# First and fourth weight sums of an FFN quad by accumulating transfers, in two down parts as well

## The chip, the cores and the metric

One core of a Trainium2 chip runs the whole program. The time is device microseconds of one execution. Before the change it is 1014.78 us, the median of three runs (1014.74 to 1015.67).

## The reference

One layer of an encoder on 512 tokens of width 1024, all in float32: an input projection, two token mixers (a short gated convolution and a retention in both directions), a merge, and a SwiGLU FFN. The change lies in the FFN:

```
h2 = rmsnorm(x, g_ffn)
x = x + (silu(h2 @ w_ff_gate) * (h2 @ w_ff_up)) @ w_ff_down      # D_FF = 2816
return rmsnorm(x, g_final)
```

## The kernel before, in words

**Products.** A matrix product is done as three TensorE products of a high and a low part (fp32r), since each float32 number is split into a rounded high part and the rest. Weights are split on the way: ScalarE casts the high part (line 208, tile `whi`), VectorE subtracts it from the number and leaves the low part (line 209, tile `wlo`). Most large products are moreover done in Strassen's form by Winograd: the weight is cut in four quarters b11, b12, b21, b22, and seven products take the place of eight. Four of the seven need sums of quarters, one made from the other: t1 = b11+b12, t2 = t1+b22, t4 = t2+b21, and t3 = b12+b22. The token side has such forms too (a11, a12, a22, s1 to s4).

**The FFN.** Its 2816 columns are 11 blocks of 256. Ten of them are taken as five gate-and-up quads, `("g", 0)` to `("g", 4)`, which hold two blocks of gate and two of up; the eleventh is `("f", 10)`, the lone block. The down projection runs in three parts, `("d", 0)` and `("d", 4)` after quads 2 and 4, and `("d", 8)` at the end. `plan` writes the order of all weight units by hand: quads 0 and 1, quad 2, down part 0, quads 3 and 4, down part 4, the lone block, down part 8.

**Units and look-ahead.** A form of a quad comes in two units (u = 0 and 2), each of 128x1024 numbers, and each unit feeds 12 matmuls of 128x512. A quad or a down part of four thus has 14 units. `take` hands the next unit to TensorE's code and prepares units until two are ready. `load_raws` issues the loads of raw quarters on SP four units ahead into ten buffers (`raw`); `prefetch_form` makes the sum and the split. There are five buffers each of high and low parts, so that no split is made more than some four units ahead of TensorE. The queues are in order each, but the framework may place ready work of a later line ahead of earlier lines.

**Sums.** A sum is made in place in the raw buffer. VectorE does it at line 307. For quads 1 to 4, the sums t3 and t4 are instead made by an accumulating transfer: `late` notes it, and `join_late` (line 321) lets POOL issue it one unit later; the transfer adds the quarter in DRAM to the raw buffer. It must wait until the buffer's former contents have been split. For quad 0 and the output projection (`SUMMED`) all sums are prepared in DRAM far ahead.

**Orders.** `FORMS` is the order b11, t1, t2, b21, t3, t4, b22; `DOWN_FORMS` takes b21 second. In a quad, `first_a` does b11's product, `first_b` b21's, and `rest` the others, with b21's product in its middle unless `middle=False`. After the product of t3's first unit a quad calls `behind`, which makes the token-side forms of the quad before for the down part (`forms_of`, `act_forms_of`); that function returns `others`, which makes the last four of those splits. `gated` (lines 1228 to 1233) applies silu and the product of gate and up and transposes; line 1298 and its like subtract parts. `scatter` writes a quad's results to the layout of the down part with 16 transfers on SP.

**Down parts.** `down` runs `strassen(..., early=True)`. Its results of part 0 go to DRAM (`put_first`) and are added to the residual in DRAM by POOL in `add_first`, which is written ahead of down part 4 and waits for quad 4 by way of a small POOL operation, `mark` (line 1349). Part 4's results are added in DRAM by POOL (`add_y`, line 1309).

**Lone block.** `fm_quad` does its seven products in the order a11, s1, s2, a12, s3, a22, s4 and calls `ev11` after the fourth, `ev22` after the fifth. ev11 calls `behind()()`, which makes all of quad 4's token forms.

Of the kernel before, what the change touches and what calls it, by code (L numbers as in the profile page):

```python
# [39 lines left out]
NQ = NFB // 2  # L40

FF_PARTS = ((0, 4), (4, 4), (8, 3))
# [12 lines left out]
WIDTH = {"w": 512, "x": 256, "a": 512, "o": 512, "f": 256, "g": 512, "d": 512}  # L55
FORMS = ("b11", "t1", "t2", "b21", "t3", "t4", "b22")

DOWN_FORMS = ("b11", "b21", "t1", "t2", "t3", "t4", "b22")

NEEDS = {"b11": "b11", "b21": "b21", "t1": "b12", "t2": "b22"}  # L60

def plan():

    out = []

    def a(name, col):
        out.append(("c", name, 0, 8, col, 256))

    def b(name, row, nk, col, nc):
        out.append(("c", name, row, nk, col, nc))

    def quad(c0, c1):
        for name in FORMS:  # L80
            for u in (0, 2):
                out.append(("q", ("w", c0, c1), name, u, 2))

    for h in range(EARLY):
        for r in (0, 512):
            b("w_in", r, 4, (C_Q + h * QK, C_K + h * QK), 512)
    for h in range(HEADS):
        quad(C_V + h * VD, C_G + h * VD)
        if h >= EARLY:
            a("w_in", C_Q + h * QK)  # L90
            a("w_in", C_K + h * QK)
    for c in (0, 512):
        quad(C_GA + c, C_GR + c)
    for c0, c1 in ((C_XC, C_GC), (C_XC + 256, C_GC + 256), (C_GB, C_GB + 256)):
        for name in FORMS:
            out.append(("q", ("x", c0, c1), name, 0, 4))
    for s in (2, 3):
        for c in (C_XC, C_GC, C_GB):
            a("w_in", c + s * 256)
    for h in range(HEADS):  # L100
        for c in (0, 512):
            b("w_r_out", h * VD, 4, c, 512)
    for kind, name in [("a", x) for x in FORMS[:6]] + [("o", "b11"), ("a", "b22")] + [
            ("o", x) for x in ("t1", "t2", "b21", "b22", "t3", "t4")]:
        for u in (0, 2):
            out.append(("q", (kind,), name, u, 2))
    def f(q, *names):
        for n in names:
            if q == LONE:
                out.append(("q", ("f", q), n, 0, 4))  # L110
            else:
                for u in (0, 2):
                    out.append(("q", ("g", q), n, u, 2))

    def d(q0, n):
        names = FORMS if q0 + n == NQ else DOWN_FORMS
        units = [(name, u) for name in names for u in range(0, n, 2)]
        if q0 + n == NQ:

            i = units.index(("b21", 2))  # L120
            units[i:i + 3] = units[i + 1:i + 3] + units[i:i + 1]
        for name, u in units:
            out.append(("q", ("d", q0), name, u, min(2, n - u)))

    f(0, "b11", "b21")
    f(1, "b11")
    f(0, "t2", "t1", "t3", "t4", "b22")
    f(1, "t1", "t2", "b21", "t3", "t4", "b22")
    f(2, *FORMS)
    d(*FF_PARTS[0])  # L130
    f(3, *FORMS)
    f(4, *FORMS)
    d(*FF_PARTS[1])
    f(LONE, *FORMS)
    d(*FF_PARTS[2])
    return out

# [8 lines left out]
SUMMED = (("g", 0), ("o",))  # L146


def joined(quad, name):

    return quad[0] == "g" and quad not in SUMMED and name in ("t3", "t4")


def parts(quad):
# [3 lines left out]
def loads():  # L158


    out = []
    for i, x in enumerate(PLAN):
        if x[0] == "q":
            _, quad, name, u, nk = x
            need = name if quad in SUMMED else NEEDS.get(name)
            if need:
                out.append((i, quad, need, u, nk * WIDTH[quad[0]]))
    return out + [(len(PLAN), quad, "b12", u, QH) for quad in SUMMED for u in parts(quad)]
# [7 lines left out]
def block_kernel(ctx: ExitStack, tc: tile.TileContext, xw0, xw, xT, xtok, wpack, wquad, cols, decs, rot, g_ffn, g_final, out):  # L176
# [50 lines left out]
    pos = [0]  # L227
# [32 lines left out]
    def quarter(quad, name, u):  # L260
        return wquad[next(i for i, x in enumerate(QUARTERS) if x[1:4] == (quad, name, u))]
# [34 lines left out]
    def prefetch_form(quad, f, u, nk):  # L296


        n = nk * WIDTH[quad[0]]
        if quad in SUMMED:  # L300
            here, more = f, None
        else:
            here = {"t1": "b11", "t2": "b11", "t4": "b11", "t3": "b12"}.get(f, f)
            more = {"t1": "b12", "t2": "b22", "t4": "b21", "t3": "b22"}.get(f)
        t = raws[quad, here, u][:, 0:n]
        if more and not joined(quad, f):
            nc.vector.tensor_tensor(out=t, in0=t, in1=raws[quad, more, u][:, 0:n], op=ALU.add)  # L307
        hi, lo = unit()
        split(t, hi[:, 0:n], lo[:, 0:n])
        for g, after, src, add in (("t3", "t1", "b12", "b22"), ("t4", "t2", "b11", "b21")):  # L310
            if f == after and joined(quad, g):
                late.append((pos[0] + 1, raws[quad, src, u], quarter(quad, add, u), n))
        return [(hi, lo)]

    late = []
# [771 lines left out]
    def behind(i):  # L1087
        if i == 5:
            turn(0, 0)
            return  # L1090
        turn(1, 1)
        po["a"] = [bank(), bank()]
        prod_tm(4, of(M["a11"]), po["a"], True, False, lambda tt: join(tt, 0, po["a"][tt]))
        turn(0, 1)
        form(M, "s1", m32["a22"], m32["a21"], m32["a22"], ALU.subtract)
        form(M, "s2", m32["a22"], m32["a22"], m32["a11"], ALU.subtract)
# [100 lines left out]
    def lone_gated(th, g, u):  # L1197

        s = t512()
        nc.scalar.activation(s, g, AF.Silu)  # L1200
        if not lone_x:
            lone_x.extend(t512().rearrange("p (b q e t) -> p b q e t", b=2, q=1, e=2) for _ in range(2))
        for b, o in enumerate(lone_x):
            for e in range(2):
                x, y = (t.rearrange("p (e j b r) -> p e b j r", e=2, j=2, b=4)[:, e, 2 * b:2 * b + 2] for t in (u, s))
                z = o[:, :, 0, e, 64 * th:64 * th + 64].rearrange("p b (j r) -> p b j r", j=2)
                nc.vector.tensor_tensor(out=z, in0=x, in1=y, op=ALU.mult)
# [3 lines left out]
    def lone(behind):  # L1211
        got = {}

        def ev11(t):
            got.update(g=t)
            behind()()
        forms = {"a11": XF[0, 0], "a12": XF[1, 0], "a22": XF[1, 1], **{n: XF[n] for n in ("s1", "s2", "s3", "s4")}}
        fm_quad(forms, ev11, lambda ps: lone_gated(1, ps, got["u"]),
                lambda t: got.update(u=t), lambda t: lone_gated(0, got["g"], t))
        act_forms_of(LONE, 1, *lone_x)()  # L1220

    turned = {}
# [41 lines left out]
    def first_b(i):  # L1264
        b = [bank(), bank()]
        prod_tm(4, of(XF[1, 0]), b, True, True)
        for tt, p1 in enumerate(heads_of[i][1]):
            nc.vector.tensor_tensor(out=p1, in0=b[tt], in1=p1, op=ALU.add)
# [32 lines left out]
    def quad(i, behind, after=None):  # L1301
        first_a(i)
        if after:
            after()
        rest(i, behind=behind)

    first = dram.tile([S, D], F32, name="first_part")
    def add_y(t, nb, half):
# [221 lines left out]
```

## Time and profile before

| | before |
| --- | --- |
| median of three runs | 1014.78 us (1014.74 to 1015.67) |
| the profiled execution | 1016.66 us, its span 1014.4 us |
| TensorE busy | 1002.5 us, 99% |
| VectorE busy | 894.2 us, 88% |
| ScalarE busy | 547.4 us, 54% |
| GpSimd (POOL) busy | 154.3 us, 15% |
| moved by DMA | 215.87 MB, mean 213 GB/s |
| granted TensorE clock | 0.996 |

In the profile's rows a timeline line has start, duration (both us), engine, source line, operation, out<-in tiles, shapes, the count of merged instructions and, in brackets, the idle time before it and what ended it. A line of a stretch (A:B) has the length, then the busy time and count of TensorE, its weight loads, VectorE, ScalarE and POOL, then the granted clock, the mean busy share of the 16 DMA engines and GB/s. A group of issues has the least, middle and largest duration in ns, and the first and last start.

### The profile page before, as it was taken

The page shows a single profiled execution, that of the slowest core. Times are in us where ns is not written, and L with a number is a line of the kernel's source. Part 1 is how long each engine was busy: PE and PEld are TensorE (multiplying, and loading weights), DVE is VectorE, ACT ScalarE, POOL GpSimd, SP SyncE. Part 2 cuts the span into 40 slices and gives each one's busy share as a digit, 9 for nine tenths or more (in the row PEclk, how much of TensorE's full clock was granted, in tenths as well). Part 3 has the DMA queues.
Part 4 walks back from the last instruction along what each step waited for, and adds up shares of the span by engine and source line. Part 5 has one row for each costly group of instructions (what it writes and reads, how often), then busy time and mean ns, then how long its engine had stood idle before and what let it go on. Part 6 is the DMA issues. An engine that isn't in the chain of part 4 may idle for free.

```text
span 1014.4 us, 13342 instructions
## 1 busy us (share of the span) xinstructions
PE 1002.5 (99%) x4746; PEld 838.4 (83%) x4746; DVE 894.2 (88%) x1163; ACT 547.4 (54%) x736; POOL 154.3 (15%) x246
## 2 busy tenths in 40 slices
PE   9999999999999999999999999999999999999996
PEld 7888888888888998888888888888887888888884
DVE  7878898979798888697989997999988996989897
ACT  7547655553655455343452325577665555574664
POOL 0030221222122004112221200011101000003202
PEclk9999999999999999999999999999999999999998
DMA  9525587695767658839687865467677369486953
GB/s 352 189 76 184 185 289 219 206 306 177 231 191 257 222 217 276 332 131 331 154 306 257 288 233 180 127 202 231 167 228 152 139 208 267 107 248 127 274 140 104
DMA packets 60642, 215.87 MB, mean 213 GB/s; under 512 B 8928, under 2 KB 9056, under 8 KB 55968
## 3 DMA queue, kind: packets, MB, share of 16 engines
q1 hardware_dynamic: 42592, 144.73, 41.7%
q0 software_dynamic: 17696, 70.01, 25.6%
q8 instruction: 37, 0.61, 0.3%
q10 hardware_dynamic: 288, 0.29, 0.1%
q14 instruction: 29, 0.24, 0.1%
HBM read 171.21 MB, written 57.41 MB: 225 GB/s over the span
## 4 chain that ended last, share of the span: by engine, by line
PE 87%; DVE 8%; issue 2%; SPq 2%; DMA 1%; ACT 1%; POOL 0%; POOLq 0%; DVEq 0%; ACTq 0%
PE bank L445 48%; PE bank L360 10%; PE bank L361 10%; PE bank L362 10%; PE bank L401 8%; DVE wlo L209 2%; SPq L1243 2%; DVE raw L307 1%; DMA big<-turned 1%; DVE turned L1233 1%; DVE t L1229 1%; DVE t L1182 0%; DVE big L209 0%; PE bank L501 0%; ACT whi L208 0%
## 5 line engine op out<-in xcount | busy, mean ns | idle before, releaser
L208 ACT CAST whi<-raw 128x1024 fp32r<-128x1024 f32 (+2 forms) x299 | 301.8, 1028 | 239.0 <-PE bank L445 73.5
L209 DVE TENSOR_TENSOR wlo<-raw,whi 128x1024 fp32r<-128x1024 f32 (+2 forms) x300 | 350.8, 1189 | 69.6 <-ACT whi L208 68.9
L445 PE MATMUL bank<-whi,xform 128*128 128x512 f32 x1056 | 330.5, 390 | 0.0
L445 PEld LDWEIGHTS bank<-whi,xform 128*128 128x128 f32 x1056 | 198.0, 188 | 42.2 <-DVE xform L209 1.0
L445 PE MATMUL bank<-wlo,xform 128*128 128x512 f32 x528 | 205.8, 390 | 0.5 <-DVE wlo L209 0.5
L445 PE MATMUL bank<-whi,big 128*128 128x512 f32 x596 | 187.5, 390 | 0.3 <-ACT t L452 0.3
L307 DVE TENSOR_TENSOR raw<-raw 128x1024 f32<-128x1024 f32 x112 | 132.2, 1198 | 0.8
L445 PEld LDWEIGHTS bank<-whi,big 128*128 128x128 f32 x596 | 111.7, 188 | 24.5 <-ACT t L452 1.1
L445 PEld LDWEIGHTS bank<-wlo,xform 128*128 128x128 f32 x528 | 99.1, 188 | 22.1 <-DVE wlo L209 1.7
L445 PE MATMUL bank<-wlo,big 128*128 128x512 f32 x298 | 116.1, 390 | 0.1
L452 ACT COPY t<-bank 128x512 f32<-128x512 f32 x95 | 55.5, 587 | 70.8 <-PE bank L445 55.8
L360 PE MATMUL bank<-big,whi 128*128 128x512 f32 x220 | 85.7, 390 | 0.0
L362 PE MATMUL bank<-big,wlo 128*128 128x512 f32 x220 | 85.6, 389 | 0.0
L361 PE MATMUL bank<-big,whi 128*128 128x512 f32 x220 | 85.6, 389 | 0.0
L445 PEld LDWEIGHTS bank<-wlo,big 128*128 128x128 f32 x298 | 55.9, 188 | 12.0 <-DVE wlo L209 0.6
L401 PE MATMUL bank<-xform,whi 128*128 128x256 f32 x304 | 55.3, 283 | 0.2 <-ACT t L452 0.2
L360 PE MATMUL bank<-whi,big 128*128 128x512 f32 x128 | 49.8, 389 | 0.0
L361 PE MATMUL bank<-wlo,big 128*128 128x512 f32 x128 | 49.8, 389 | 0.0
L362 PE MATMUL bank<-whi,big 128*128 128x512 f32 x128 | 49.8, 389 | 0.0
L362 PEld LDWEIGHTS bank<-big,wlo 128*128 128x128 f32 x220 | 41.3, 188 | 8.7
L361 PEld LDWEIGHTS bank<-big,whi 128*128 128x128 f32 x220 | 41.3, 188 | 8.5
L360 PEld LDWEIGHTS bank<-big,whi 128*128 128x128 f32 x220 | 41.3, 188 | 8.5
(211 smaller groups left out, 1395.1 us busy)
## 6 DMA issues: line engine op xcount, KB each, us to landing
raw<-wquad SPq DMA_DIRECT2D x140, 512.0 KB, 5.2
raw<-wpack SPq DMA_DIRECT2D x42, 512.0 KB, 5.9
raw<-wquad POOLq DMA_DIRECT2D x16, 512.0 KB, 6.4
t_g<-wquad POOLq DMA_DIRECT2D x12, 512.0 KB, 7.7
z<-t POOLq DMA_DIRECT2D x24, 256.0 KB, 5.6
t_o<-wquad POOLq DMA_DIRECT2D x12, 512.0 KB, 6.7
zform<-z POOLq DMA_DIRECT2D x6, 1024.0 KB, 7.1
big<-turned SPq DMA_DIRECT2D x80, 64.0 KB, 4.5
```

Of the source, the lines that this page charges most:

```text
L208: first = (round or nc.scalar.copy)(hi, src)
L209: low_of[0] = nc.vector.tensor_tensor(out=lo, in0=src, in1=hi.bitcast(F32), op=ALU.subtract)
L307: nc.vector.tensor_tensor(out=t, in0=t, in1=raws[quad, more, u][:, 0:n], op=ALU.add)
L360: nc.tensor.matmul(ps, lh, rh, start=first, stop=False)
L361: nc.tensor.matmul(ps, lh, rl, start=False, stop=False)
L362: nc.tensor.matmul(ps, ll, rh, start=False, stop=last)
L401: nc.tensor.matmul(o, l[:, c], r[:, k], start=start and s == 0 and k == 0 and i == 0, stop=stop and k == 3 and i == 2, skip_group_check=True)
L445: nc.tensor.matmul(pss[tt], l, r[:, c], start=start and k == 0 and i == 0, stop=stop and k == n - 1 and i == 2, skip_group_check=True)
L452: nc.scalar.copy(t, ps)
L1229: nc.vector.tensor_tensor(out=s, in0=u, in1=s, op=ALU.mult)
L1233: nc.vector.transpose(t[:, :, :, j, :].rearrange("p q i r -> p i q r"), s.rearrange("p (i q c) -> p i q c", i=4, q=4)[:, :, 2 * h:2 * h + ...
L1243: nc.sync.dma_start(o[32 * q:32 * q + 32], turned[i][q // 2][32 * b:32 * b + 32, q % 2].rearrange("c i j r -> c (i j r)"))
```

## The change

For quads 1 to 4 the transfers now make t1 (b12 added to b11 after b11's split) and t4, and VectorE makes t2 and t3. The quarter b12 is loaded only for t3. The two down parts 0 and 4 do the same; before, VectorE made all their sums. Quads 2, 3 and 4 take b21 second, so `quad` calls `first_b` right after `first_a`, and its sums with the first product follow there. In the lone block the last four token forms of quad 4 are made at `ev22`, one product later than before.

```
-DOWN_FORMS = ("b11", "b21", "t1", "t2", "t3", "t4", "b22")
+EARLY_FORMS = ("b11", "b21", "t1", "t2", "t3", "t4", "b22")
+NEEDS_JOINED = {"b11": "b11", "b21": "b21", "t2": "b22", "t3": "b12"}
...
-    f(2, *FORMS)
+    f(2, *EARLY_FORMS)
     d(*FF_PARTS[0])
-    f(3, *FORMS)
-    f(4, *FORMS)
+    f(3, *EARLY_FORMS)
+    f(4, *EARLY_FORMS)
...
-def joined(quad, name):
-    return quad[0] == "g" and quad not in SUMMED and name in ("t3", "t4")
+def joined(quad):
+    return quad not in SUMMED and (quad[0] == "g" or quad[0] == "d" and quad[1] < FF_PARTS[-1][0])
+
+def needed(quad, name):
+    return NEEDS_JOINED.get(name) if joined(quad) else name if quad in SUMMED else NEEDS.get(name)
...
-        if more and not joined(quad, f):
+        if more and not (joined(quad) and f in ("t1", "t4")):
             nc.vector.tensor_tensor(out=t, in0=t, in1=raws[quad, more, u][:, 0:n], op=ALU.add)
         hi, lo = unit()
         split(t, hi[:, 0:n], lo[:, 0:n])
-        for g, after, src, add in (("t3", "t1", "b12", "b22"), ("t4", "t2", "b11", "b21")):
-            if f == after and joined(quad, g):
-                late.append((pos[0] + 1, raws[quad, src, u], quarter(quad, add, u), n))
+        add = {"b11": "b12", "t2": "b21"}.get(f)
+        if add and joined(quad):
+            late.append((pos[0] + 1, raws[quad, "b11", u], quarter(quad, add, u), n))
...
         def ev11(t):
-            got.update(g=t)
-            behind()()
+            got.update(g=t, others=behind())
...
-                lambda t: got.update(u=t), lambda t: lone_gated(0, got["g"], t))
+                lambda t: (got.update(u=t), got["others"]()), lambda t: lone_gated(0, got["g"], t))
...
         first_a(i)
         if after:
             after()
-        rest(i, behind=behind)
+        first_b(i)
+        rest(i, middle=False, behind=behind)
```

More of the change, by code (lines that the diff above doesn't have):

```diff
@@ L115, in d @@
     def d(q0, n):
-        names = FORMS if q0 + n == NQ else DOWN_FORMS
+        names = FORMS if q0 + n == NQ else EARLY_FORMS
         units = [(name, u) for name in names for u in range(0, n, 2)]
@@ L164, in loads @@
             _, quad, name, u, nk = x
-            need = name if quad in SUMMED else NEEDS.get(name)
+            need = needed(quad, name)
             if need:
```

## The prediction

> **What bounds the kernel now.** I read the page first: the busy shares, and the chain that ended last.
>
> ```profile
> span 1014.4 us, 13342 instructions
> PE 1002.5 (99%) x4746; PEld 838.4 (83%) x4746; DVE 894.2 (88%) x1163; ACT 547.4 (54%) x736; POOL 154.3 (15%) x246
> PE 87%; DVE 8%; issue 2%; SPq 2%; DMA 1%; ACT 1%; POOL 0%; POOLq 0%; DVEq 0%; ACTq 0%
> ```
>
> TensorE is busy for all but 12 us, and most of those lie before the first product and after the last. The chain still gives VectorE 8%. Which of the two sets the pace in the FFN is not seen from busy time, because matmuls are pipelined and their ends are modelled. It is seen from the distance between the starts of neighbouring matmuls. So I went through the timeline of TensorE from 691 us (first FFN product) to the end, looking for starts that lie too far apart. Undisturbed, three 128x512 matmuls take 0.68 us, 0.227 us each (770.14 to 770.82 below), and one unit of weights (12 matmuls) takes 2.72 us. In the stretch that the change touches there are four places where the starts lie further apart:
>
> ```profile
> 767.72 0.61 PE L445 MATMUL bank<-whi,xform 128*128 128x512 f32 x2
> 768.42 0.50 PE L445 MATMUL bank<-wlo,xform 128*128 128x512 f32 x1
> 768.75 0.63 PE L445 MATMUL bank<-whi,xform 128*128 128x512 f32 x2
> ...
> 770.14 0.61 PE L445 MATMUL bank<-whi,xform 128*128 128x512 f32 x2
> 770.59 0.39 PE L445 MATMUL bank<-wlo,xform 128*128 128x512 f32 x1
> 770.82 0.61 PE L445 MATMUL bank<-whi,xform 128*128 128x512 f32 x2
> 771.89 0.50 PE L445 MATMUL bank<-wlo,xform 128*128 128x512 f32 x1 [0.46 <-DVE wlo L209]
> 772.23 0.63 PE L445 MATMUL bank<-whi,xform 128*128 128x512 f32 x2
> ...
> 824.62 0.39 PE L445 MATMUL bank<-whi,big 128*128 128x512 f32 x1
> 825.32 0.50 PE L445 MATMUL bank<-whi,big 128*128 128x512 f32 x1 [0.31 <-ACT t L452]
> 825.65 0.40 PE L445 MATMUL bank<-wlo,big 128*128 128x512 f32 x1
> ...
> 886.44 0.61 PE L445 MATMUL bank<-whi,xform 128*128 128x512 f32 x2
> 887.00 0.50 PE L445 MATMUL bank<-wlo,xform 128*128 128x512 f32 x1
> 887.34 0.64 PE L445 MATMUL bank<-whi,xform 128*128 128x512 f32 x2
> ...
> 939.76 0.83 PE L445 MATMUL bank<-whi,big 128*128 128x512 f32 x2
> 940.43 0.40 PE L445 MATMUL bank<-wlo,big 128*128 128x512 f32 x1
> ```
>
> A row of x2 takes 0.45 us from its start to the next start, a row of x1 0.227. Quad 2: 0.70 for two (+0.25), 0.33 for one (+0.10), 1.07 for two (+0.62), 0.34 for one (+0.11): 1.08 us lost. Down part 0: 0.70 and 0.33 for one each, 0.57 lost. Quad 4: 0.56 for two and 0.34 for one, 0.22 lost. Down part 4: 0.67 for two, 0.22 lost. Together 2.09 us, and that is all that the quads 1 to 4 and the two down parts can return; the rest of the FFN before the last evictions runs at 0.227 us a matmul, and the change removes no matmul.
>
> Who is late in quad 2? VectorE, and it has no gap:
>
> ```profile
> 761.21 1.18 DVE L209 TENSOR_TENSOR wlo<-raw,whi 128x1024 fp32r<-128x1024 f32 x1
> 762.31 1.21 DVE L307 TENSOR_TENSOR raw<-raw 128x1024 f32<-128x1024 f32 x1
> 763.44 1.28 DVE L1298 TENSOR_TENSOR t<-bank,t 128x512 f32<-128x512 f32 x2
> ...
> 767.18 1.18 DVE L209 TENSOR_TENSOR wlo<-raw,whi 128x1024 fp32r<-128x1024 f32 x1
> 768.29 2.35 DVE L307 TENSOR_TENSOR raw<-raw 128x1024 f32<-128x1024 f32 x2
> 770.61 2.36 DVE L209 TENSOR_TENSOR wlo<-raw,whi 128x1024 fp32r<-128x1024 f32 x2
> ```
>
> L307 is the weight sum, L209 the low part of a split. Before the low part that TensorE awaits (the first of the two at 770.61, done at 771.8) stand three sums (762.31 and two at 768.29: t1's two halves and t2's first) and the eviction of the quad before. The three sums take 3.5 us.
>
> In the down parts it is ScalarE's order. A cast that waits for a sum stands between the two copies that free the banks for the next product:
>
> ```profile
> 822.32 0.59 ACT L452 COPY t<-bank 128x512 f32<-128x512 f32 x1 [2.06 <-PE bank L445]
> 823.73 1.05 ACT L208 CAST whi<-raw 128x1024 fp32r<-128x1024 f32 x1 [0.82 <-DVE raw L307]
> 824.68 0.58 ACT L452 COPY t<-bank 128x512 f32<-128x512 f32 x1
> 939.46 0.58 ACT L452 COPY t<-bank 128x512 f32<-128x512 f32 x1
> ```
>
> **The change, part by part.**
>
> Sums in the down parts. A quad of weights has four sums of two halves each. Down parts 0 and 4 go from eight VectorE sums each to four; their t1 and t4 come by transfer. Eight sums of 1.2 us, 9.6 us of VectorE, go, and with them what the cast at 823.73 and its like in down part 4 waited for. t1's two sums are done before t2's, so t2's splits too come some 2.3 us earlier. I count the 0.57 and the 0.22 as gone.
>
> Sums in quads 1 to 4. The number stays four on VectorE, four by transfer, but t2 and t3 are now VectorE's instead of t1 and t2, and b21 goes to the place of t1. In quad 2 that takes the three sums out from before the low part at 770.61: it could be done at 771.8-3.5 = 768.3, and TensorE wants it at the third matmul of its unit, 770.7 undisturbed. 2.4 us of margin where 1.1 was missing. What comes in: the two sums of first products (`first_b`, 0.6 us each as at L1298) move up to b21's end, but those wait for that product and so stand behind this low part. Quad 4 has the same order. I count 1.08 and 0.22 as gone. The t3 sums fall later, where each unit brings VectorE one low part and one sum, 2.4 us in 2.72; that is cover with little to spare, and without it they would cost what they overrun.
>
> The transfers. There were 16; now there are 24. POOL issues them and they land:
>
> ```profile
> L321 POOL DMA_DIRECT2D raw<-wquad x16: 870/873/947, 721.1 to 892.0; - x16
> DMA to landing us min/median/max: 5.3/6.4/11.2
> ```
>
> Eight more cost POOL 7 us, in which nothing of the path stands on it. Each starts when both parts of a split are done and must land before the next cast of the same buffer. This distance shrinks from six units (16.3 us) to four (10.9 us). The tightest by the rows above is t1's second half in quad 2: the low part ends at 762.4, the landing is at 767.7 to 773.6, the cast ends by 774.6 and the low part by 775.8; TensorE reaches the unit at 767.95+3x2.72 = 776.1. Even the slowest landing seen fits, by 0.3 us; with 6.4 us there are 5 us to spare. Cost zero, and 0 to 3 us for the worst case below.
>
> A page of the Trainium skill speaks against these transfers. "SBUF — State Buffer", section "A bandwidth-pool intuition that's wrong (but worth ruling out)", says that descriptors of a GpSimd-issued DMA cannot be written while VectorE holds the shared port, and gives 620 ns alone against 3100 ns beside a VectorE copy; by that ratio the issue would take 4.4 us (estimate from the page), each landing would come 3.5 us later, and quad 2's margin would be mostly used up, a gain nearer 1 us than 2. The trace does not agree for the operations here: all 16 issues took 0.870 to 0.947 us, between 721 and 892 us, where VectorE had few gaps. The chance of late landings below takes nothing from it.
>
> Loads. The loads on SP keep their number and size; b12 moves from t1's place to t3's and the b21 load forward. By the order of uses a buffer is free at least six units (16.3 us) before it is wanted in both versions. Cost zero; the bound is a unit, 2.7 us, if a load should fall behind the 16 issues of a `scatter`.
>
> Lone block. The rest of quad 4's forms (four splits and two differences) move from after its fourth product to after its fifth. It is no less work: six operations of 0.6 us, 3.6 us of VectorE, move behind that product, against splits and sums of the last down part that can come forward.
>
> ```profile
> 969.58 0.63 PE L445 MATMUL bank<-whi,big 128*128 128x512 f32 x2
> 970.41 0.50 PE L401 MATMUL bank<-xform,whi 128*128 128x256 f32 x2 [0.21 <-ACT t L452]
> 980.00:1000.00 20.00, 20.00 (x89) 16.39 (x88) 19.27 (x32) 13.21 (x24) 3.91 (x6) 1.00 0.35 53
> ```
>
> I take zero on the path, between -0.4 (TensorE waits for a copy at 969.58, 0.83 us for two matmuls instead of 0.45, and matmuls of the last down part could fill that) and +1, of which below.
>
> Sum: -1.08 -0.57 -0.22 -0.22 = -2.1 us against the profiled execution (span 1014.4 of 1016.66 us). It is a difference of stalls, so it carries over to the median: 1014.78-2.1 = 1012.7 us. Its own range comes from the lone block's -0.4 to +1 and from a 0.22 that may stay: 1012.3 to 1013.9.
>
> **The rivals.**
>
> Given back in the down parts. If ScalarE's order keeps t4's cast between the two copies, the cast now waits for a landing instead of a sum. In down part 4 the DMA engines are full then, and the low part before the transfer is this:
>
> ```profile
> 928.00:936.00 8.00, 8.00 (x37) 6.64 (x36) 8.00 (x9) 4.11 (x4) 1.79 (x2) 1.00 1.11 213
> 931.52 1.22 DVE L209 TENSOR_TENSOR wlo<-raw,whi 128x1024 fp32r<-128x1024 f32 x1
> ```
>
> It ends at 932.7, or 930.4 without t1's sums; plus 5.3 to 11.2 us the landing is at 935.7 to 941.6, the cast ends by 942.7 at the latest and the copy by 943.2 instead of 940.0. Lost: 0 to 3.2 us, so 1012.7 to 1015.9. For it: the DMA share of 1.11. Against it: with the median landing nothing is lost.
>
> Slower, through POOL's queue. In down part 4, t1's second transfer is written in the program behind the mark and the eight additions of the first part:
>
> ```profile
> 920.11 0.22 POOL L1349 TENSOR_SCALAR mark<-t 128x1 f32<-128x1 f32 x1 [27.20 <-DVE t L1229]
> 920.39 6.81 POOL L1309 DMA_DIRECT2D ydr<-first_part  x8
> 915.30 2.31 DVE L209 TENSOR_TENSOR wlo<-raw,whi 128x1024 fp32r<-128x1024 f32 x2
> 930.24 0.62 PE L445 MATMUL bank<-whi,big 128*128 128x512 f32 x2
> ```
>
> If the queue keeps that order, the transfer starts at 927.2 instead of 916.5 (its low part is the first at 915.30), lands at 933.6 (6.4) to 938.4 (11.2), and the cast ends 1.05 later. TensorE wants that unit at 930.46, at 928.6 with the gain: 6.1 to 10.9 us lost, 4 to 9 net, 1018.8 to 1023.7 us. It decides as soon as the issue comes after about 925. Against it: the queues are not in program order throughout (at 768.29 t2's first sum runs ahead of a split of t1), and the transfer is ready 3.6 us before the mark.
>
> The lone block's forms collide. VectorE is full there (19.27 of 20 us in the stretch from 980), so 3.6 us of forms for which nothing comes forward push the splits of the last down part; I let one us of that reach TensorE: 1013.7 us.
>
> Nothing happens: other work of VectorE moves into the place of the sums and TensorE waits as before, 1014.8.
>
> **How the numbers follow.** 0.2% is 2 us, about what a measurement of this kernel can tell from no change; the forecast gain sits on that line. Forecast 0.56 (0.35 of it below 1012.75), given back 0.19 (0.04 of it over 1016.8), POOL's queue 0.11, lone block 0.09, nothing 0.05. So faster 0.36 and 0.02 for a lone block that gains, 0.38; slower 0.15; within 0.47. The range leaves out POOL's queue and the far end of the giving back above, 0.13, and 0.05 below: 1011.9 to 1016.8.
>
> **What would show it.** Right: starts of matmuls 0.227 us apart through quad 2's third and fourth unit and through t3 of both down parts; sums at L307 eight fewer (112 to 104) and accumulating transfers 24; casts of t1 and t4 that wait for nothing or for a landing well ahead of TensorE; the mark on POOL behind all of t1's transfers. Wrong: a gap of TensorE that ends on a ScalarE copy with a cast waiting for a DMA ahead of it, a transfer behind the mark, or gaps in the last down part at 984 to 990 us.

## The result, and the profile after

The change is slower: 1044.03 us, the median of five runs (1040.49 to 1046.08), against 1015.27 us before (1014.74 to 1015.91). The ratio is 1.028, 95% interval 1.026 to 1.030. The prediction was 1012.7 us. The profiled execution of the change took 1040.49 us, its span 1038.7 us, 24.3 us more than the span before; it is the shortest of the five, and where the others lost up to 5.6 us more isn't seen here. Below, lines of the changed kernel are six higher than before (those from 1228 to 1298 are five higher): the sum L307 is L313, the cast L208 is L214, the low part L209 is L215, the accumulating transfer L321 is L327, TensorE's product L445 is L451, the copy out of a bank L452 is L458.

The page of the changed kernel, the group of the sums, and the waits of TensorE (line, whom it waited for: us in all, times, longest) come first, then the transfers' issues and landings:

```profile
span 1038.7 us, 13368 instructions
PE 1005.9 (97%) x4746; PEld 841.4 (81%) x4746; DVE 886.6 (85%) x1155; ACT 546.9 (53%) x736; POOL 161.4 (16%) x254
PE 75%; DVE 9%; issue 7%; DMA 6%; POOL 2%; ACT 1%; SPq 0%; POOLq 0%; DVEq 0%; ACTq 0%
L313 DVE TENSOR_TENSOR raw<-raw 128x1024 f32<-128x1024 f32 x104 | 122.6, 1198 | 4.7 <-DMA raw<-wquad 3.9
...
PE bank L451 <- ACT t L458: 21.8, 4, 11.7
...
L327 POOL DMA_DIRECT2D raw<-wquad x24: 872/873/1011, 691.7 to 944.1; - x24
  ACT whi L214: 54.8, 15
DMA to landing us min/median/max: 5.3/6.4/15.6
```

The work did what the diff says: 104 sums, 24 transfers. But the chain that ended last is 75% TensorE instead of 87%, DMA has 6% of it instead of 1%, and TensorE waits four times, 21.8 us in all, for the copy at L458 that frees a bank. ScalarE, which makes that copy, waited 54.8 us for the transfers. Summing every distance between TensorE's starts beyond the undisturbed one gives some 7 us before and 31 us after; the 24 us between them are the whole loss of the profiled execution.

TensorE at the first and the last of the four places (an undisturbed start follows 0.227 us after the one before):

```profile
783.56 0.39 PE L451 MATMUL bank<-whi,xform 128*128 128x512 f32 x1
789.40 0.79 PE L451 MATMUL bank<-whi,xform 128*128 128x512 f32 x1 [5.45 <-ACT t L458]
...
949.32 0.39 PE L451 MATMUL bank<-whi,big 128*128 128x512 f32 x1
961.36 0.80 PE L451 MATMUL bank<-whi,big 128*128 128x512 f32 x1 [11.65 <-ACT t L458]
```

783.56 and 949.32 are the last matmuls of t2's product in quad 2 and in down part 4. ScalarE's timeline at the four places (quad 2, down part 0, quad 4, down part 4), and then in quad 3, where nothing is lost:

```profile
783.54 1.04 ACT L214 CAST whi<-raw 128x1024 fp32r<-128x1024 f32 x1 [1.21 <-DMA raw<-wquad]
784.49 1.56 ACT L214 CAST big<-big 128x1024 fp32r<-128x1024 f32 x2
787.81 1.04 ACT L214 CAST whi<-raw 128x1024 fp32r<-128x1024 f32 x1 [1.76 <-DMA raw<-wquad]
788.76 1.06 ACT L458 COPY t<-bank 128x512 f32<-128x512 f32 x2
...
827.25 1.05 ACT L214 CAST whi<-raw 128x1024 fp32r<-128x1024 f32 x1 [4.12 <-DMA raw<-wquad]
831.75 1.04 ACT L214 CAST whi<-raw 128x1024 fp32r<-128x1024 f32 x1 [3.44 <-DMA raw<-wquad]
832.70 1.07 ACT L458 COPY t<-bank 128x512 f32<-128x512 f32 x2
...
905.60 1.05 ACT L214 CAST whi<-raw 128x1024 fp32r<-128x1024 f32 x1 [2.82 <-DMA raw<-wquad]
906.56 1.05 ACT L214 CAST big<-big 128x1024 fp32r<-128x1024 f32 x1
909.23 0.62 ACT L214 CAST big<-big 128x512 fp32r<-128x512 f32 x1 [1.63 <-DMA big<-turned]
909.76 1.04 ACT L214 CAST whi<-raw 128x1024 fp32r<-128x1024 f32 x1
910.71 1.06 ACT L458 COPY t<-bank 128x512 f32<-128x512 f32 x2
...
955.96 1.04 ACT L214 CAST whi<-raw 128x1024 fp32r<-128x1024 f32 x1 [13.27 <-DMA raw<-wquad]
959.78 1.04 ACT L214 CAST whi<-raw 128x1024 fp32r<-128x1024 f32 x1 [2.77 <-DMA raw<-wquad]
960.73 1.06 ACT L458 COPY t<-bank 128x512 f32<-128x512 f32 x2
...
869.04 1.06 ACT L214 CAST whi<-raw 128x1024 fp32r<-128x1024 f32 x1 [0.15 <-PE bank L451]
870.40 0.59 ACT L458 COPY t<-bank 128x512 f32<-128x512 f32 x1 [0.30 <-PE bank L451]
```

At each of the four places the two casts `whi<-raw` are t4's two units, in quad 3 the cast is the second of them (the casts of `big` are token forms). On ScalarE they stand ahead of the two copies that empty the banks of t2's product. The copies are due when that product ends; the cast ahead of them waits for the landing, and the queue is in order. In quad 3 the cast waited for no landing and the copy came on time.

Quad 4 is a mixed case. t4's second transfer landed there at 908.90, before t2's product ended. Its cast at 909.76 waited for no landing, but stood behind the cast of a token form at 909.23, which waited for quad 3's scattered results. The slowest of those 16 transfers took 6.8 us to land, against at most 3.3 us in the kernel without t4's transfer (below). The copies stood behind both casts.

The transfer starts behind t2's split. Its low parts on VectorE (the second of three, the second of four) and the issues on POOL:

```profile
776.56 3.48 DVE L215 TENSOR_TENSOR wlo<-raw,whi 128x1024 fp32r<-128x1024 f32 x3
941.34 4.62 DVE L215 TENSOR_TENSOR wlo<-raw,whi 128x1024 fp32r<-128x1024 f32 x4
...
779.26 0.89 POOL L327 DMA_DIRECT2D raw<-wquad  x1 [0.24 <-issue]
927.33 0.87 POOL L327 DMA_DIRECT2D raw<-wquad  x1 [3.61 <-DVE wlo L215]
930.37 0.22 POOL L1355 TENSOR_SCALAR mark<-t 128x1 f32<-128x1 f32 x1 [2.17 <-DVE t L1234]
944.09 0.89 POOL L327 DMA_DIRECT2D raw<-wquad  x1 [0.17 <-issue]
```

Worked out from the timelines of VectorE, POOL, ScalarE and TensorE, for t2's and t4's second unit at each place (us):

| | low part of t2 done | t4's transfer issued | t4's cast starts | last start of t2's product | next start | lost |
| --- | --- | --- | --- | --- | --- | --- |
| quad 2 | 778.90 | 779.26 | 787.81 | 783.56 | 789.40 | 5.61 |
| down part 0 | 822.35 | 822.70 | 831.75 | 829.77 | 833.33 | 3.33 |
| quad 3 | 860.62 | 861.11 | 869.04 | 871.33 | 871.56 | 0 |
| quad 4 | 901.23 | 901.58 | 909.76 | 909.41 | 911.33 | 1.69 |
| down part 4 | 943.69 | 944.09 | 959.78 | 949.32 | 961.36 | 11.81 |

At all four places with a loss TensorE goes on 1.57 to 1.59 us after t4's cast starts: the cast and one copy. So the transfer's deadline is not the use of t4 by TensorE, four units on. It is the end of t2's product, 4.3 to 7.8 us after the issue at the four places and 10.2 us in quad 3. The landings took 8.5 us in quad 2, 8.9 in down part 0, 7.3 in quad 4, 15.6 in down part 4, and 7.1 in quad 3.

How much would have been lost without the copies behind the casts? As an estimate from the table: TensorE wants t4's second unit three units (8.2 us) after t2's product ends, which is 0.23 us after its last start. That is 792.0 in quad 2, where the cast ended at 788.9, and 957.7 in down part 4, where it ended at 960.8. So t4 itself was late for TensorE in down part 4 alone, by some 3 of the 11.8 us.

### The profile page after: what moved, and what is told of

It is laid out like the page before. It is cut to its first block, busy times and chain, and to the rows that moved or that the text cites. A ratio compares the mean times of both kernels' runs of the same rounds, so it can differ in the third digit from the quotient of the medians.

```text
span 1038.7 us, 13368 instructions
## 1 busy us (share of the span) xinstructions
PE 1005.9 (97%) x4746; PEld 841.4 (81%) x4746; DVE 886.6 (85%) x1155; ACT 546.9 (53%) x736; POOL 161.4 (16%) x254
## 4 chain that ended last, share of the span: by engine, by line
PE 75%; DVE 9%; issue 7%; DMA 6%; POOL 2%; ACT 1%; SPq 0%; POOLq 0%; DVEq 0%; ACTq 0%
PE bank L451 39%; PE bank L366 10%; PE bank L368 10%; PE bank L367 10%; PE bank L407 6%; DMA raw<-wquad 6%; DVE wlo L215 3%; DVE raw L313 1%; DVE big L215 1%; DVE t L1188 1%; POOL ydr L1315 1%; ACT whi L214 1%; POOL raw L327 1%; DVE t L1294 0%; PE bank L507 0%
## 5 line engine op out<-in xcount | busy, mean ns | idle before, releaser
L214 ACT CAST whi<-raw 128x1024 fp32r<-128x1024 f32 (+2 forms) x299 | 303.9, 1029 | 297.8 <-PE bank L451 87.6
L215 DVE TENSOR_TENSOR wlo<-raw,whi 128x1024 fp32r<-128x1024 f32 (+2 forms) x300 | 351.9, 1189 | 101.0 <-ACT whi L214 100.6
L451 PE MATMUL bank<-whi,xform 128*128 128x512 f32 x1056 | 332.8, 392 | 7.0 <-ACT t L458 7.0
L451 PEld LDWEIGHTS bank<-whi,xform 128*128 128x128 f32 x1056 | 199.3, 189 | 50.3 <-ACT t L458 7.8
L451 PE MATMUL bank<-wlo,xform 128*128 128x512 f32 x528 | 206.5, 391 | 0.0
L451 PE MATMUL bank<-whi,big 128*128 128x512 f32 x596 | 189.3, 392 | 15.1 <-ACT t L458 14.8
L451 PEld LDWEIGHTS bank<-whi,big 128*128 128x128 f32 x596 | 112.8, 189 | 40.0 <-ACT t L458 15.7
L313 DVE TENSOR_TENSOR raw<-raw 128x1024 f32<-128x1024 f32 x104 | 122.6, 1198 | 4.7 <-DMA raw<-wquad 3.9
L451 PE MATMUL bank<-wlo,big 128*128 128x512 f32 x298 | 116.9, 392 | 0.0
L451 PEld LDWEIGHTS bank<-wlo,xform 128*128 128x128 f32 x528 | 99.7, 189 | 20.6
L458 ACT COPY t<-bank 128x512 f32<-128x512 f32 x95 | 54.8, 586 | 50.7 <-PE bank L451 32.7
L451 PEld LDWEIGHTS bank<-wlo,big 128*128 128x128 f32 x298 | 56.4, 189 | 11.8 <-DVE wlo L215 0.3
L327 POOL DMA_DIRECT2D raw<-wquad x24 | 21.2, 884 | 220.9 <-DVE wlo L215 209.4
L367 PEld LDWEIGHTS bank<-big,whi 128*128 128x128 f32 x220 | 41.3, 188 | 8.6
```

What stands on the lines that cost most here:

```text
L214: first = (round or nc.scalar.copy)(hi, src)
L215: low_of[0] = nc.vector.tensor_tensor(out=lo, in0=src, in1=hi.bitcast(F32), op=ALU.subtract)
L327: nc.gpsimd.dma_start(out=t[:, 0:n], in_=src[:, 0:n], accum_op=ALU.add)
L367: nc.tensor.matmul(ps, lh, rl, start=False, stop=False)
L451: nc.tensor.matmul(pss[tt], l, r[:, c], start=start and k == 0 and i == 0, stop=stop and k == n - 1 and i == 2, skip_group_check=True)
L458: nc.scalar.copy(t, ps)
```

## Experiments

Ratios are to the kernel before on the same chip, with their 95% interval. Two theories stood against each other; the letters in the expectations name variants of them, each with what it means. One: t4's transfer is issued too late for the place of its casts on ScalarE. Two: something else of the change is at fault (the transfers as such, the order of the quads, the queue of POOL, the lone block).

**Without t4's transfer.** t1 stays with the transfers, t4 goes back to VectorE.

```
-        if more and not (joined(quad) and f in ("t1", "t4")):
+        if more and not (joined(quad) and f == "t1"):
-        add = {"b11": "b12", "t2": "b21"}.get(f)
+        add = {"b11": "b12"}.get(f)
```

> The changed kernel with t1 alone made by transfer, in quads 1 to 4 and in the two down parts; t2, t3 and t4 are VectorE's. The number of VectorE's sums is then 12 higher than in the changed kernel and 4 higher than before. Theory A: no cast waits for a transfer in front of a copy with TensorE behind it, 1013 to 1017 us (some VectorE lateness may return). Theory D (t1's transfer, with 10.9 us from split to next cast, does the harm): 1030 us or more.

1014.25 us, ratio 0.9986 (0.9977 to 0.9996), 30 us below the change and as theory A had it. Its page:

```profile
span 1011.4 us, 13343 instructions
PE 97%; DVE 1%; issue 0%; ACT 0%; POOL 0%; POOLq 0%; DVEq 0%; ACTq 0%
```

The chain is 97% TensorE where it was 87%. In the quads and the two down parts no distance of TensorE's starts is over the undisturbed one by more than 0.2 us: the four stalls of before are gone, and t1's twelve transfers cost nothing. The whole loss hangs on t4's transfer: without it there is none.

**The order of the quads, with the transfers of before.** The kernel before, its quads 2 to 4 in the new order; t3 and t4 by transfer there, no transfers in the down parts.

```
-    f(2, *FORMS)
+    f(2, *DOWN_FORMS)
...
-        rest(i, behind=behind)
+        first_b(i)
+        rest(i, middle=False, behind=behind)
```

> The kernel before, with b21 second in quads 2 to 4 and its product early, as in the change; the transfers stay those of before (t3 and t4 in the quads alone), the lone block too. Theory E: t4 has four units instead of six and loses as in the kernel with the quads alone (6.5 us in quad 2, 2.2 to 2.7 in the others): 1022 to 1030 us. If t4's distance is not at fault but t1's transfer ahead of it: 1012 to 1016 us.

1028.37 us, ratio 1.0116 (1.0101 to 1.0132). TensorE's waits:

```profile
PE bank L445 <- ACT t L452: 10.6, 2, 5.9
```

6.0 us in quad 2, 4.8 in quad 4, at the same place. So in the quads it is the order that does it, without t1's transfer and without any in the down parts: with b21 taken second, t4 follows t2 two units sooner, and a transfer of t4 behind which TensorE did not stop at six units' distance stops it at four.

**The quads alone.** `joined` holds for quads only; the down parts make all sums on VectorE.

```
-    return quad not in SUMMED and (quad[0] == "g" or quad[0] == "d" and quad[1] < FF_PARTS[-1][0])
+    return quad not in SUMMED and quad[0] == "g"
```

> The changed kernel with the two down parts' sums back on VectorE; quads 1 to 4 and the lone block as changed. Theory A: the gaps in down part 0 and 4 (3.3 and 11.8, with the slow matmuls behind the second 1.5 more) go back to the 0.6 and 0.2 of before, those in quads 2 and 4 stay: about 1040.5-3.5-13.3+0.8 = 1024.5 us, 1022 to 1029. If the down parts were all of it: 1015. If the shorter distance in the quads were all of it: 1040.

1028.53 us, ratio 1.0127 (1.0111 to 1.0143). Losses of 6.5, 2.7 and 2.2 us in quads 2, 3 and 4, none in the down parts. The loss splits into about 13 us for the quads and 15 for the down parts. There the order is that of before; what is new in them is the transfer.

**Less on the DMA engines.** The mark and the eight additions of the first part are written behind down part 4.

```
-    add_first(nc.gpsimd.tensor_scalar_add(mark, gate_of[0][:, 0:1], 0.0))
     down(4, add_y)
+    add_first(nc.gpsimd.tensor_scalar_add(mark, gate_of[0][:, 0:1], 0.0))
```

> The changed kernel with the eight additions of the first part's result written behind down part 4 instead of ahead of it. Theory A with the DMA engines' crowd as the reason for the slow landings in down part 4 (12.9 and 15.6 us from issue, against 5.3 to 9.1 elsewhere): the landings fall to about 9, the gap of 11.8 us to about 5, and 1 us of slow matmuls goes: 1033 to 1037 us, with the gaps in quads 2 and 4 and down part 0 unchanged. If the loads and the scatter on the other queue make the crowd: 1040 to 1046, the landings as before.

1038.77 us, ratio 1.0228 (1.0212 to 1.0244). The two landings of t4 in down part 4 (issues at 943.5 and 944.7):

```profile
DMA to landing us min/median/max: 8.9/9.9/10.8
```

In the change they took 12.9 and 15.6 us. The loss there falls from 11.8 to 6.6 us; the other places stay (6.1, 3.3, 1.8), and a new 1.4 us appears in the last part. A landing 4.8 us shorter gives a loss 5.2 us smaller: the landing sets it. The time lies above the 1033 to 1037 us expected, since the gap fell to 6.6 us and not to 5.

**An earlier start.** t4's buffer is that of b21, and b21 is added to it right behind b21's split, four units before t2's. It leaves out t4's true sum, so its result is not the layer's; it serves for the time alone.

```
-            here = {"t1": "b11", "t2": "b11", "t4": "b11", "t3": "b12"}.get(f, f)
+            here = {"t1": "b11", "t2": "b11", "t4": "b21" if joined(quad) else "b11", "t3": "b12"}.get(f, f)
...
-        add = {"b11": "b12", "t2": "b21"}.get(f)
+        add = {"b11": "b12", "b21": "b21"}.get(f)
...
-            late.append((pos[0] + 1, raws[quad, "b11", u], quarter(quad, add, u), n))
+            late.append((pos[0] + 1, raws[quad, f, u], quarter(quad, add, u), n))
```

> The changed kernel with t4's transfer made early: it adds b21 to the raw buffer of b21 as soon as that is split, eight units ahead of t4's cast, instead of to t2 after t2's split. So t4's weights are 2 x b21 and not t4; sums on VectorE, transfers, their sizes and the order of products stay those of the changed kernel. Theory H (the harm is only that t4's landing comes after its cast's place in ScalarE's queue): no gap, 1013 to 1017 us. Theory C (24 transfers, or t4's by whatever start, crowd the DMA engines): 1030 us or more.

1026.68 us, ratio 1.0104 (1.0090 to 1.0117): between the ranges of the two theories, so neither holds alone. 17 us are back, down part 0 and quads 3 and 4 without a loss over 0.25 us. Left are 2.9 us in quad 2, where ahead of the copies stand t3's second cast, which waits for VectorE's sum, and t4's two behind it, and 4.6 us in down part 4. POOL and ScalarE there:

```profile
922.13 0.22 POOL L1355 TENSOR_SCALAR mark<-t 128x1 f32<-128x1 f32 x1 [1.14 <-DVE t L1234]
922.41 5.95 POOL L1315 DMA_DIRECT2D ydr<-first_part  x7
931.02 0.91 POOL L327 DMA_DIRECT2D raw<-wquad  x1 [0.40 <-DVE t L471]
...
944.73 1.04 ACT L214 CAST whi<-raw 128x1024 fp32r<-128x1024 f32 x1 [6.58 <-DMA raw<-wquad]
945.68 1.06 ACT L458 COPY t<-bank 128x512 f32<-128x512 f32 x2
```

Here the second transfer stands behind the mark and the additions on POOL, starts at 931.02 and lands 13.6 us later. That is the mechanism of the prediction's rival of POOL's queue, for t4 instead of t1.

**A later use.** In quads 2 to 4 and the down parts t4 changes places with b22, form and product.

```
-EARLY_FORMS = ("b11", "b21", "t1", "t2", "t3", "t4", "b22")
+EARLY_FORMS = ("b11", "b21", "t1", "t2", "t3", "b22", "t4")
...
```

> The changed kernel with the order b11, b21, t1, t2, t3, b22, t4 in quads 2 to 4 and in down parts 0 and 4: the product of t4 comes last, so that its transfer has six units (16.3 us) after t2's split instead of four (10.9). Theory E (the loss is the short time from t2's split, itself only 1 to 5 us ahead of TensorE, to t4's cast; ScalarE's queue only decides which copy stands behind it): the gaps in quad 2, down part 0 and quad 4 go, down part 4 keeps up to 6 us of its 11.8 since its landings took 13 to 16 us: 1013 to 1022 us. Theory F (a t4 transfer does the same harm wherever its product stands, since the framework places its cast just as early): 1030 us or more.

1036.55 us, ratio 1.0199 (1.0177 to 1.0220). Its waits, and ScalarE in down part 4:

```profile
PE bank L451 <- ACT t L458: 10.9, 2, 8.8
...
953.76 1.04 ACT L214 CAST whi<-raw 128x1024 fp32r<-128x1024 f32 x1 [6.17 <-DMA raw<-wquad]
959.61 1.04 ACT L214 CAST whi<-raw 128x1024 fp32r<-128x1024 f32 x1 [4.80 <-DMA raw<-wquad]
960.57 1.07 ACT L458 COPY t<-bank 128x512 f32<-128x512 f32 x2
```

This is theory F's range; E had 1013 to 1022 us. Two units (5.4 us) more give only 7.5 us back in all. In down part 4 t4's casts now stand ahead of the copies of t3's product instead of t2's, and TensorE loses 8.9 us there: the same wait, one product on. In quads 2 to 4 it waits three times, 4.0 us in all, for a subtraction of VectorE (L1303 there): it empties the bank of t1's product, which the exchanged order wants one product sooner. So this edit moves more than t4.

**The casts off ScalarE's queue.** t4's high part is made by POOL.

```
-        split(t, hi[:, 0:n], lo[:, 0:n])
+        split(t, hi[:, 0:n], lo[:, 0:n], round=nc.gpsimd.tensor_copy if f == "t4" and joined(quad) else None)
```

> The changed kernel with the casts of t4's units (quads 1 to 4, down parts 0 and 4) on POOL instead of ScalarE; transfers and their times as in the changed kernel. Theory H: ScalarE's copies wait for no landing any more; the gaps after t2's product in quad 2, down part 0 and quad 4 go; VectorE's low part still waits for the landing, in front of evictions one product later, and in down part 4 t4 itself is up to 5 us late: 1015 to 1024 us. Theory I (t4 is late for TensorE itself, whatever queue waits): 1030 us or more.

1031.63 us, ratio 1.0147 (1.0131 to 1.0162): 12 us back, yet outside theory H's 1015 to 1024.

```profile
PE bank L451 <- ACT t L458: 5.7, 2, 3.7
PE bank L451 <- POOL whi L214: 1.2, 1, 1.2
...
907.15 0.62 ACT L214 CAST big<-big 128x512 fp32r<-128x512 f32 x1 [8.03 <-DMA big<-turned]
907.68 1.07 ACT L458 COPY t<-bank 128x512 f32<-128x512 f32 x2
```

Down part 4 falls from 11.8 us to 1.4 and 1.0 at two places, though its landings took 12.4 and 14.4 us, only 0.6 and 1.2 less than in the change. So most of the 11.8 us was the wait in ScalarE's queue. The 2.4 us left are TensorE waiting for t4 itself, first for POOL's cast and then for VectorE's low part; the estimate above had 3. But the copies in quad 4 and down part 0 now stand behind another cast that waits for a DMA, a token form that waits for the scattered results (3.8 and 2.2 us lost), and 1.9 us are lost in quad 2 and 1.8 in the last part.

**The casts held behind the copies.** t4's split may start only behind the last copy out of a bank written before it; `last_copy` is noted where the copy is made. The same line was tried in four kernels more.

```
+        if f == "t4" and quad[0] in "gd" and quad not in SUMMED and quad[1] < FF_PARTS[-1][0]:
+            with tc.issue_after(last_copy[0].ins):
+                split(t, hi[:, 0:n], lo[:, 0:n])
...
```

> The changed kernel with one order added: on ScalarE the casts of t4's units stand behind the copies that free the banks of t2's product. Theory A (the loss is ScalarE's queue: t4's casts wait for their transfers in front of those copies): the gaps of TensorE after t2's product in quad 2 (5.6 us), down part 0 (3.3), quad 4 (1.7) and down part 4 (11.8) go, except that in down part 4 the second landing (at 959.7 in the changed kernel, where t4's second unit was due at 957.5) may still cost up to 4: 1012.5 to 1018 us, at or below the kernel before. Theory B (the transfers themselves are too slow, whatever stands behind them: t4 is late for TensorE): TensorE stops at t4 instead, 1030 us or more. Theory C (the added traffic slows the loads): 1035 to 1045 us.

> The kernel with t1 alone by transfer, and t4's casts held behind the copies of t2's product. With t1 alone TensorE loses no more than 0.2 us at one place in the quads and down parts, so there is nothing left to win there: 1014.25 give or take 0.7. A look for a version under both.

> The kernel before the change, with nothing changed but that t4's casts of quads 1 to 4 and of down parts 0 and 4 are held behind the copies of t2's product. Theory G: the gaps of 0.57 and 0.22 us in the down parts, where a copy stands behind a cast that waits for a sum, go: 1014.5 to 1015 against 1015.3. If other orders change with it, within 1 us of that.

> The kernel with t1 and t3 by transfer, and t4's casts (which wait for a sum of VectorE there) held behind the copies of t2's product. Theory G: the one gap of that kernel (3.3 us in quad 2, in front of a copy with a cast of t4 ahead of it) goes, 1018.23 to about 1014.5; if the late landings of t1 in quad 2 hold VectorE back by themselves, the gap moves one product on and 1017 to 1018 stays.

> The kernel with t4's product last (six units after t2's split), and t4's casts on ScalarE held behind the last copies written before them, here those of t3's product. Theory G (both count: the landing must come before TensorE wants t4, and the cast must not stand in ScalarE's queue ahead of a copy that is due before that landing): the gaps of the kernel with t4 two units later (2.3 and 1.1 in quad 2, 1.2 in quad 3, 2.3 in quad 4, 8.9 in down part 4) shrink to what a late landing costs by itself, some 3 us in down part 4: 1015 to 1022 us against 1036.55. Theory F (a t4 transfer harms wherever its cast stands): 1030 us or more.

| | without the line | with it |
| --- | --- | --- |
| the change | 1.0280 (1.0259 to 1.0302) | 1.0286 (1.0257 to 1.0315) |
| without t4's transfer | 0.9986 (0.9977 to 0.9996) | 1.0077 (1.0063 to 1.0092) |
| before | 1 | 0.9994 (0.9985 to 1.0003) |
| t1 and t3 by transfer (below) | 1.0021 (1.0012 to 1.0030) | 1.0078 (1.0065 to 1.0091) |
| t4 two units later | 1.0199 (1.0177 to 1.0220) | 1.0241 (1.0226 to 1.0255) |

Of the five forecasts with the line only that for the kernel before came true (1015.03 us); the others measured 1043.47 us (theory A: 1012.5 to 1018), 1024.01 (1014.25), 1022.97 (1014.5, or 1017 to 1018) and 1039.38 (1015 to 1022). The test is inconclusive. The line costs 9 us in the kernel without t4's transfer, where no transfer is late, though nothing in the kernel before: the held-back casts pile up, and later copies and products wait for them. The waits of the kernel without t4's transfer but with the line, where L451 has become L456 and L1297 copies the banks of t3's product:

```profile
PE bank L456 <- ACT whi L214: 5.2, 3, 2.0
PE bank L456 <- ACT t L1297: 2.9, 3, 1.0
```

In the change with the line, t4's transfers of down part 4 were issued at 947.39 and 949.20 and landed at 961.88 and 964.18; the casts now stood ahead of the copies of t3's product, and TensorE lost 11.5 us there, one product on. So the line can't tell how much of the loss is the late landing and how much the place of the casts.

**Another pair by transfer.** t1 and t3: a transfer adds b12 to b11 for t1; b12 is also loaded, at t1's place, and another transfer adds b22 to it for t3. t2 and t4 are VectorE's.

```
...
-        add = {"b11": "b12", "t2": "b21"}.get(f)
+        to, add = {"b11": ("b11", "b12"), "t1": ("b12", "b22")}.get(f, (None, None))
```

> The changed kernel with t1 and t3 by transfer (t3: b22 added to b12 as soon as that is loaded, which waits for no split) and t2 and t4 on VectorE, in quads 1 to 4 and both down parts: as many sums on VectorE and as many transfers as in the changed kernel. Theory E: no transfer hangs on t2's split, so no gap: 1011.5 to 1014.5 us, at or a little under t1 alone (1014.25), which has 12 sums more on VectorE. Theory C (24 transfers crowd the DMA engines): 1018 us or more.

1018.23 us, ratio 1.0021 (1.0012 to 1.0030). Theory E had 1011.5 to 1014.5 us, so it missed, and theory C's 1018 is just reached. But there are as many transfers as in the change, 24, and 26 us less: their number does not make the loss. One loss is left:

```profile
PE bank L451 <- ACT t L458: 2.9, 1, 2.9
```

It lies in quad 2, where a cast of t4 waits for VectorE's sum ahead of the copies. Here t1's transfers are late: those of quad 2 landed at 767.84 and 770.71, after 7.2 and 8.9 us, and VectorE, whose low parts wait for t1's casts, stood idle for 3.5 us between 765 and 775 us. Without t3's transfer they landed by 764.50, VectorE was busy throughout that stretch, and nothing was lost.

**The lone block as before.** ev11 calls `behind()()` again, in the last kernel and in the one without t4's transfer.

> The kernel with t1 and t3 by transfer, with the lone block as before (all of quad 4's token forms after the fourth product). It measures the lone block's part of the change: 0, between -1 (the move costs: this kernel is the faster) and +0.4 (the move pays) against its neighbour with the move. Theory E does not depend on it: 1011.5 to 1014.5 us.

> The kernel with t1 alone by transfer, with the lone block as before. It measures the lone block's part where nothing else is late: against 1014.25 with the move, 0, between -0.7 and +0.7. If it is the faster of the two, it is the version to keep.

1017.51 us, ratio 1.0015 (1.0006 to 1.0024), against 1018.23; and 1013.95 us, ratio 0.9981 (0.9972 to 0.9989), against 1014.25. The differences, 0.7 and 0.3 us, are within the intervals. The latter kernel, t1 alone by transfer and the lone block as before, has the lowest time of all, 1.9 us below before (1.1 to 2.8).

## Why the prediction was wrong, point by point

- *The four stalls go (-2.1 us).* Right. Without t4's transfer they are gone, and the kernel is 1.4 us faster than before with the lone block's move and 1.9 us without it. That ScalarE's order makes those in the down parts is also seen in the kernel before with t4's casts held behind the copies: there the stalls of both down parts are gone, and those of quads 2 and 4 stay. (In the margin for quad 2, 767.95 is the second start of the unit, not the first, 767.72; that shifts it by 0.2 us and changes nothing.)
- *The transfers: "Cost zero, and 0 to 3 us for the worst case".* This is the step that failed. It took the tightest margin to be t1's in quad 2. For TensorE t1's did hold, though VectorE stood idle for 2.6 us before t1's second low part there, since that transfer landed at 769.65. t4's was worked out only in a rival, for down part 4. The step gave every transfer until the cast of its buffer is wanted by TensorE, four units, where t4's must land by the end of t2's product, because ScalarE's queue holds t4's casts ahead of that product's copies. The term put at zero cost 22.4 us of waiting at four places and some 4.4 us of slow matmuls behind two of them. In quads 2 to 4 the new order took two units from just this transfer; in the down parts the transfer is new. Its start hangs on t2's split, which is only 2 to 6 us ahead of TensorE at the four places.
- *The rival "given back in the down parts": 0 to 3.2 us in down part 4.* The right mechanism, a cast waiting for a landing between TensorE and its copy, with the wrong size and at one place of four. That its middle value cost nothing rested on the median landing; the chance given to it was 0.19. Down part 4 lost 11.8 us. The 8.6 us between come from three numbers, on the clock of before (the change ran 10.93 us later there, from TensorE's start of t2's second unit, 946.83 against 935.90). The working used the low part of t2's first unit, 930.4, where the second transfer counts, issued at 944.09-10.93 = 933.16: 2.8 us. The landing took 15.6 us, not 11.2 at most: 4.4 us. And the working put t4's cast between the two copies, where both casts stood ahead of both: so TensorE waited for the first bank, wanted at 949.55-10.93 = 938.6, and not for the second, free at 940.0: 1.4 us. That t2's splits would come 2.3 us earlier was right: the second low part ended at 943.69-10.93 = 932.8 against 935.0 before. The rival left out down part 0, and no rival had quads 2 and 4.
- *POOL's queue.* It did not happen in the change: t1's last transfer was issued at 927.33, ahead of the mark at 930.37. It was seen once, for t4, with the earlier start.
- *Loads, the lone block, the issues.* No loss is seen there. The kernels without the lone block's move are 0.3 and 0.7 us faster, not told from zero. The Trainium skill ("SBUF — State Buffer", section "A bandwidth-pool intuition that's wrong (but worth ruling out)") gives its slow case for a GpSimd DMA beside a VectorE copy. VectorE's sums and low parts here are TENSOR_TENSOR operations; 24 issues took 0.872 to 1.011 us each beside a VectorE busy 85% of the span, so the slow case is not seen.
- *What would show it wrong: "a gap of TensorE that ends on a ScalarE copy with a cast waiting for a DMA ahead of it".* That is what the rows above show.

Open: how the loss would divide if the copies could be had ahead of the casts at no cost (only the kernel with POOL's casts tells something, for down part 4), and why 2.9 us stay in quad 2 with the earlier start of t4's transfer: that a cast waits for its sum is seen, not why the sum is late. How much of quad 4's 1.7 us is the token form's late landing was not tried by itself.

## What to carry to other kernels

A transfer's deadline is where its reader stands in its engine's queue, not where the result is used: look for what is queued behind the reader and when that is due. When an order is changed, work out the margin again for every transfer whose two ends move closer, beginning with the one whose start depends on the latest producer; here moving one form took 5.4 us from t4's transfer in the quads and cost some 13 us, and the same transfer, new in the down parts, cost some 15. Take a landing time from the stretch where the transfer will run: a median of 6.4 us says little where the DMA engines are full.

## What the runs showed of the hardware

Stretches of the changed kernel (length, then busy time and count of TensorE, its weight loads, VectorE, ScalarE, POOL, then the granted clock, DMA share and GB/s):

```profile
789.40:795.00 5.60, 5.60 (x14) 4.45 (x15) 4.19 (x5) 1.50 (x3) 0.00 (x0) 0.54 0.58 191
833.30:839.00 5.70, 5.67 (x25) 4.69 (x26) 3.50 (x4) 3.05 (x4) 0.00 (x0) 1.00 0.32 79
940.00:950.00 10.00, 9.71 (x43) 7.70 (x41) 5.96 (x7) 2.25 (x3) 3.62 (x4) 1.00 1.11 218
961.30:966.50 5.20, 5.14 (x15) 4.11 (x16) 2.00 (x2) 1.75 (x4) 0.00 (x0) 0.62 0.42 136
```

**The clock halves behind some waits.** Behind the gaps of 5.6 and 11.8 us the mean granted clock was 0.54 and 0.62 in the stretches above: it was 0.50 until 794.5 and 965.2, and matmuls started 0.43 us apart for 5.1 and 3.8 us. These two stalls thus cost 2.5 and 1.9 us more than their length. Behind the gap of 3.3 us, at 833.30, the clock was 1.00. But the length of a gap does not decide it: in the kernel with the additions moved away a gap of 3.3 us in down part 0 was followed by a clock of 0.50 from 834.2 to 837.5 us, and in the kernel with t4 two units later one of 2.3 us in quad 4 by 0.50 from 913.4 to 916.7. The Trainium skill ("TensorE: Matmul & The Clock Gate", section "Part 1: The HAM clock gate (the "warmup" mystery)") has the clock halved after an idle window of about 3.4 us and restored after about 3.4 us of activity in windows that run freely. The trace does not agree on the first, since gaps of 2.3 and 3.3 us were enough. The 3.8 and 5.1 us fit the second, if the first window after the gap was already under way.

**Accumulating transfers land late beside many other transfers.** With a DMA share of 1.11 from 940 to 950 us the two 512 KB transfers took 12.9 and 15.6 us, against a median of 6.4; with the eight additions of the first part moved away, 8.9 and 10.8. The share alone does not tell it: it was 1.03 from 943 to 953 us in that kernel too.
